# Second expert weights one step later, residual one unit earlier, in a two-block MoE kernel

## The chip, the cores and the metric

The kernel runs on one core of a Trainium2 chip. A time is the device time of one execution in microseconds (us). Three runs of the kernel before gave 2467.74, 2462.54 and 2467.64 us, median 2467.64 us. One further execution was recorded by the hardware profiler, and all rows below are of that one. A difference of less than about 0.2% (4.9 us) can't be told from none.

## The reference

256 tokens of 1024 features go through two blocks of two layers each. In block 1 a layer is a mixer (in one layer a gated delta rule beside sparse attention, in the other gated linear attention) and then a mixture of 32 experts, both with the modulation that comes from a conditioning vector. Block 2 has a token mixer of four branches and again 32 experts, with layer norms, and a residual that is scaled and shifted by rows of a table. Each token picks one of four groups and in it two of eight experts. Cut to what matters, a mixture computes:

```
def expert_block(args):
    xi, e = args
    hid = jax.nn.silu(xi @ w1[e]) * (xi @ w3[e])
    return hid @ w2[e]
yb = lax.map(expert_block, (xb, blk_exp))
y = jnp.zeros((t, d)).at[buf_tok].add(yb * buf_w[:, None])
```

w1 and w3 of an expert are its *first weights*, w2 its *second weights*. All is in float32. In block 1 an expert is 512 wide (first weights 4 MiB, second 2 MiB), in block 2 it is 256 wide (2 MiB and 1 MiB).

## The kernel before, in words

Both mixtures are the function moe (`experts_1` calls it with nf = 512 and centred false, `experts_2` with nf = 256 and centred true). The stages follow one another: mixer, experts_1, mixer, experts_1 (block 1), then mixer, experts_2, mixer, experts_2 (block 2). Every expert is computed, for the tokens that chose it, up to a fixed number of places. The 32 experts go in 11 *units*: five of two experts with 64 places each, five of four experts with 32 places, and a last one of two experts. So 128 places fill the 128 partitions in each unit.

A unit does this. `first` loads the first weights (tiles on queue SP named A); PE multiplies the gathered tokens xg with them (L1023, the *s1* matmuls, written s1(n) for unit n); ACT and DVE make the hidden row (L1026, L1027) and PE turns it (L1036) into ht. In experts_1 this comes in two steps u = 0, 1, each with half of the unit's experts; in experts_2 it is one step. `outer` loads the second weights (tiles named B), and `second` multiplies ht with them in two halves of 512 columns (L932), from which ACT takes yh (L934) and DVE yl (L935). `combine` adds yh and yl back to the tokens' rows in PSUM (L945, PT is the 0/1 matrix of places). `back` prepares that matrix and the weights ws (L953 to L961), and `fetch` gathers the tokens of a later group (L878).

All weights pass through one ring of slots of 1 MiB, taken in rotation by `scratch`; a load waits until the slot's former content has been used, and loads are issued in the order in which they are written, on SP's queue, with at most eight outstanding. In experts_1 the ring has 22 slots, in experts_2 18. `hold` takes a slot out of the rotation for as long as the stage lasts: `keep` for the gates or the residual, and in experts_1 `held` for an accumulator.

The order of loads in experts_1 before: A of step 0, A of step 1, B, all of unit n. In experts_2: A(n), then B(n-1). The unit `turn = len(units) - 2` (the last of four experts, called t below; l is the one behind it, the last) holds an If: `overfull` (L767) computes the tokens that found no place, and its branch is entered only when a count read from memory exceeds 64. Every engine passes the If, and before it SP waits for its outstanding loads. What stands ahead of the If before: in experts_2 the rest of unit t-1 (its B, both halves of second, its combine), in both the two held slots, the first weights of unit t (`begun`), two scratch slots and one for hT, and `residual`. In experts_1 `residual` makes gate rows and clears the accumulator; in experts_2 it is `residual_2`, which loads two rows of the table lnp, half a MiB each, broadcast over the partitions (L170 w<-lnp), and computes with them on DVE (L1942, L1943).

The written order is a start: a scheduler settles the order of instructions on each engine from the dependences between tiles.

Of the kernel before, what the change touches and what calls it, by code (L numbers as in the profile page):

```python
# [811 lines left out]
def moe(c, ctx, index, scale, shift, w13, w2, nf, spare, centred, residual, end):  # L812
# [19 lines left out]
    p = c.pool(ctx, "moe")  # L832
# [88 lines left out]
    prev = None  # L921
# [41 lines left out]
    def experts(unit):  # L963
        e0, ne, _ = unit
        return [e0 + i if e0 < fixed else ranks.expert(e0 + i) for i in range(ne)]

    def first(who, u):

        per = len(who) // steps_of
        return c.slots([w13(e) for e in who[u * per:u * per + per]], [128, 8, 512 if centred else 1024])  # L970

    def outer(pr, who):
        pr["w2"] = c.slots([w2(e) for e in who], [128, 2, 4 * nf])

    turn = len(units) - 2
    for g, us in enumerate(groups):
        if g:
            P, xg = nxt[:2]
        nxt = group(groups[g + 1], False) if g + 1 < len(groups) else (None, None, [])
        share = -(-len(nxt[2]) // len(us))  # L980
        for unit in us:
            e0, ne, cap = unit
            j = e0 - us[0][0]
            n = units.index(unit)
            last = n == len(units) - 1
            todo = [nxt[2].pop(0) for _ in range(min(share, len(nxt[2])))]
            pr = {"n": n, "unit": unit, "h": []}
            who = experts(unit)
            begun = None
            if n == turn:  # L990

                if centred and prev is not None:
                    outer(prev, experts(prev["unit"]))
                    second(prev, 0)
                    second(prev, 1)
                    combine(prev)
                    prev = None
                keep = c.hold(extra)
                held = None if centred else c.hold(extra)
                begun = first(who, 0)  # L1000
                room, hT = [c.scratch(), c.scratch()], c.scratch()
                hT = hT.rearrange("p (a b) -> p a b", b=256)
                out, gate = residual(mp, keep, room, held)
                count = nc.values_load(cnt[0:1, 0:1], min_val=0, max_val=E * CAP,
                                       skip_runtime_bounds_check_because="counts of tokens")
                overfull(c, sp, None if centred else c.tok, scale, shift, out, w, pos, count, nf, *spare, gate, room,
                         hT, ranks)
                c.loaded = None
                who = experts(unit)
            if last:  # L1010
                c.ordered = True
            pr["yh"] = p.tile([128, 2, 512], F32R, name="yh", tag="yy", bufs=2)
            pr["yl"] = p.tile([128, 2, 512], F32R, name="yl", tag="yy", bufs=2)
            per = ne // steps_of
            for u in range(steps_of):
                ws = begun if begun is not None and u == 0 else first(who, u)
                q = sp.tile([128, 512], F32, name="s1")
                for k in range(8):
                    for i in range(128 // cap):

                        m, o = (i, 0) if centred else (i // 2, i % 2)
                        e = j + u * per + m
                        nc.tensor.matmul(q[cap * i:cap * i + cap, :], xg[:, k, e * cap:(e + 1) * cap],  # L1023
                                         ws[m][:, k, 512 * o:512 * o + 512], start=k == 0, stop=k == 7)
                hid = p.tile([128, 256], F32, name="hid", bufs=2)
                nc.scalar.activation(hid, q[:, 0:256], AF.Silu)  # L1026
                nc.vector.tensor_mul(hid, hid, q[:, 256:512])  # L1027
                half = len(todo) // 2
                for f in todo[:half] if u == 0 else todo[half:]:
                    f()  # L1030
                if centred and prev is not None:
                    outer(prev, prev["who"])
                    second(prev, 0)
                q = mp.tile([128, 512], F32, name="ms")
                for ch in range(2):
                    nc.tensor.transpose(q[:, ch * 128:(ch + 1) * 128], hid[:, ch * 128:(ch + 1) * 128], c.id)  # L1036
                ht = p.tile([128, 2, 128], F32, name="ht", bufs=4)
                nc.scalar.activation(ht, q[:, 0:256].rearrange("p (a b) -> p a b", b=128), AF.Copy)
                pr["h"].append(ht)
            pr["who"] = who  # L1040
            if last and not centred:

                for t in range(2):
                    nc.vector.tensor_add(c.x[:, t], c.x[:, t], out[:, t])
            if centred:
                for f in todo[half:]:
                    f()
                if prev is not None:
                    second(prev, 1)
                back(pr, j)  # L1050
                if prev is not None:
                    combine(prev)
            else:
                outer(pr, who)
                back(pr, j)
                if last:
                    combine(prev)
                else:
                    second(pr, 0)
                    if prev is not None:  # L1060
                        combine(prev)
                    second(pr, 1)
            prev = pr
    if centred:
        outer(prev, prev["who"])
    c.ordered = False
    c.table(second(prev, 0))
    combine(prev, (0,))
# [835 lines left out]
def experts_1(c, l):  # L1904

    nc, x = c.nc, c.x
    with ExitStack() as ctx:
        def residual(mp, keep, room, held):
            dg = room[0][:, 0:512].rearrange("p (a b) -> p a b", b=128)
            for hf in range(2):  # L1910
                rows(c, dg, mp, c.mod[:, l, 40 + 4 * hf:44 + 4 * hf], keep[:, hf * 512:hf * 512 + 512], tag=("ms", 2))
            nc.gpsimd.memset(held, 0.0)
            return held.rearrange("p (t d) -> p t d", t=2), keep[:, 0:1024]

        a1 = c.a["A1"][l].rearrange("(q i) p (k c) -> q i p k c", i=2, c=1024)
        b1 = c.a["B1"][l].rearrange("(q i) p (h f c) -> q i f p h c", i=2, h=2, f=4)

        def w1_of(pr, i, j, f):
            o = (f // 2) * 512 + j * 256 + (f % 2) * 128
            return a1[bass.ds(pr, 1), i, :, :, o:o + 128].rearrange("q p k c -> p (q k) c")  # L1920

        def w2_of(pr, i, f):
            return b1[bass.ds(pr, 1), i, f].rearrange("q p h c -> p (q h) c")

        def end(room, gate, y):
            for hf in range(2):
                for t in range(2):
                    o = (2 * t + hf) * 512
                    d = room[:, o:o + 512]
                    nc.vector.tensor_mul(d, y[t][hf], gate[:, hf * 512:hf * 512 + 512])  # L1930
                    nc.vector.tensor_add(x[:, t, hf * 512:hf * 512 + 512], x[:, t, hf * 512:hf * 512 + 512], d)
        moe(c, ctx, l, c.gain, c.mod[:, l, 24:32], lambda e: expert(c.a["A1"][l], e),
            lambda e: expert(c.a["B1"][l], e), 512, (w1_of, w2_of), False, residual, end)
# [12 lines left out]
def experts_2(c, l):  # L1946

    nc, x = c.nc, c.x
    with ExitStack() as ctx:
        a2 = c.a["A2"][l].rearrange("(q i) p (k c) -> q i p k c", i=2, c=512)  # L1950
        b2 = c.a["B2"][l].rearrange("(q i) p (h f c) -> q i f p h c", i=2, h=2, f=2)

        def w1_of(pr, i, j, f):
            o = j * 256 + f * 128
            return a2[bass.ds(pr, 1), i, :, :, o:o + 128].rearrange("q p k c -> p (q k) c")

        def w2_of(pr, i, f):
            return b2[bass.ds(pr, 1), i, f].rearrange("q p h c -> p (q h) c")

        def residual(mp, keep, room, held):  # L1960
            out = keep.rearrange("p (t d) -> p t d", t=2)
            residual_2(c, [room[0][:, 0:1024], room[0][:, 1024:2048]], l, 0, out)
            return out, None

        def end(room, keep, y):
            last(c, c.pool(ctx, "post"), l, keep, y)
        o = l * 32
        moe(c, ctx, 2 + l, c.vec("lnc")[:, o:o + 8], c.vec("lnc")[:, o + 8:o + 16],
            lambda e: expert(c.a["A2"][l], e),
            lambda e: expert(c.a["B2"][l], e), 256, (w1_of, w2_of), True, residual, end)  # L1970
# [317 lines left out]
```

## Time and profile before

| what | us |
|---|---|
| median of three runs | 2467.64 |
| the profiled execution | 2457.6 |
| its span, first to last instruction | 2455.8 |
| PE busy in the span | 2159.5 |
| DVE busy | 886.6 |
| ACT busy | 749.9 |

The profiled execution is 1.8 us longer than its span. PE is TensorE, PEld its loading of weights, DVE VectorE, ACT ScalarE, SP the engine whose queue issues the loads; a q behind a name (PEq, SPq) is that engine's sequencer. A row of the timeline gives start, duration, engine, line, operation, tiles and count of records, and in brackets the idle time before it and what ended that. A matmul in float32 leaves two records. Lines are those of the kernel before; behind the change the same code stands some lines higher (L1023 is L1018, L1036 is L1025, L1942 is L1925).

### The profile page before, as it was taken

The numbers are of one execution on the slowest core, as the hardware profiler recorded it, in microseconds if no ns is written. First come the engines' busy times: TensorE is split into PE (matmuls) and PEld (weight loads), VectorE is DVE, ScalarE is ACT, GpSimd is POOL, SyncE is SP. The second block draws the span as 40 slices with busy tenths as digits, with TensorE's granted clock in tenths as the row PEclk, the third lists the DMA queues.
The fourth block names the chain that finished last, engine by engine and source line by source line (L and its number), as shares of the span: only waits on it lengthen the run. The fifth ranks groups of instructions, "written<-read, shape, count | busy, mean of one in ns | idle before, by whom it ended". The sixth has DMA issues, their size and how long they took to land. (4 is left out here: it accounts for less than half of the span.)

```text
span 2455.8 us, 32737 instructions
## 1 busy us (share of the span) xinstructions
PE 2159.5 (88%) x12546; PEld 1229.3 (50%) x12546; DVE 886.6 (36%) x1983; ACT 749.9 (31%) x1493; POOL 44.6 (2%) x48
## 2 busy tenths in 40 slices
PE   7998899987778989999777798998996899999975
PEld 4667644322224864443222287995432678974322
DVE  3864511110003763111001254973111547861113
ACT  3642311211103452221111154562221445642211
POOL 0001000000000200000000000000000000000000
PEclk8999899999989999999998998998998989989998
DMA  9976569999999356899999971555999924549995
GB/s 393 407 272 284 219 271 400 422 421 422 421 384 419 112 207 255 369 401 421 421 421 383 421 288 47 190 196 223 377 417 379 370 86 142 189 155 356 414 417 234
DMA packets 119845, 775.11 MB, mean 316 GB/s; under 512 B 14185, under 2 KB 15593, under 8 KB 35450
## 3 DMA queue, kind: packets, MB, share of 16 engines
q1 hardware_dynamic: 119674, 772.85, 78.7%
q8 instruction: 105, 1.72, 0.3%
q14 instruction: 66, 0.54, 0.1%
HBM read 771.75 MB, written 1.05 MB: 315 GB/s over the span
## 5 line engine op out<-in xcount | busy, mean ns | idle before, releaser
L1023 PE MATMUL s<-w,xg 128*32 128x512 f32 (+1 forms) x3072 | 612.8, 627 | 94.9 <-DMA w<-A 53.7
L932 PE MATMUL s<-w,ht 128*32 128x512 f32 (+1 forms) x1536 | 348.8, 603 | 38.5 <-DMA w<-B 37.3
L1023 PEld LDWEIGHTS s<-w,xg 128*32 128x32 f32 (+1 forms) x3072 | 140.9, 122 | 384.9 <-issue 265.2
L396 PE MATMUL pj<-hi,wh 128*128 128x256 f32 x864 | 242.6, 283 | 3.4 <-ACT sg L1817 2.4
L397 PE MATMUL pj<-lo,wh 128*128 128x256 f32 x864 | 242.1, 282 | 0.0
L398 PE MATMUL pj<-hi,wl 128*128 128x256 f32 x864 | 239.4, 282 | 0.0
L935 DVE SCALAR_TENSOR_TENSOR yl<-s,ws,yh 128x512 fp32r<-128x512 f32 x88 | 66.0, 750 | 434.3 <-ACT yh L934 416.4
L932 PEld LDWEIGHTS s<-w,ht 128*32 128x32 f32 (+1 forms) x1536 | 83.3, 120 | 219.5 <-issue 137.3
L391 ACT ACTIVATE wh<-w 128x512 fp32r<-128x512 f32 x248 | 154.2, 630 | 117.6 <-PE pj L397 90.4
L392 DVE TENSOR_TENSOR wl<-w,wh 128x512 fp32r<-128x512 f32 x248 | 167.2, 689 | 47.7 <-ACT wh L391 43.8
L934 ACT ACTIVATE yh<-s,ws 128x512 fp32r<-128x512 f32 x88 | 60.5, 687 | 371.6 <-PE s L932 355.4
L396 PEld LDWEIGHTS pj<-hi,wh 128*128 128x128 f32 x864 | 164.9, 191 | 10.4 <-ACT sg L1817 2.8
L398 PEld LDWEIGHTS pj<-hi,wl 128*128 128x128 f32 x864 | 163.2, 191 | 5.0 <-issue 2.1
L397 PEld LDWEIGHTS pj<-lo,wh 128*128 128x128 f32 x864 | 165.2, 191 | 0.1
L1027 DVE TENSOR_TENSOR hid<-hid,s 128x256 f32<-128x256 f32 x66 | 27.7, 420 | 361.6 <-ACT hid L1026 361.5
L1026 ACT ACTIVATE hid<-s 128x256 f32<-128x256 f32 x66 | 25.4, 384 | 430.6 <-PE s L1023 430.3
L359 DVE TENSOR_TENSOR wl<-w,wh 128x512 fp32r<-128x512 f32 (+2 forms) x164 | 111.5, 689 | 97.2 <-ACT wh L358 83.4
L358 ACT ACTIVATE wh<-w 128x512 fp32r<-128x512 f32 (+2 forms) x164 | 99.8, 615 | 112.9 <-PE pj L344 54.3
L886 ACT ACTIVATE xg<-ms,mod,gain 128x128 f32<-128x128 f32 x160 | 72.6, 458 | 170.7 <-PE ms L878 170.7
L878 PEld LDWEIGHTS ms<-P,x 128*128 128x128 f32 x640 | 82.0, 193 | 81.5 <-issue 40.9
L344 PE MATMUL pj<-wl,hi 128*128 128x512 f32 (+2 forms) x272 | 106.4, 393 | 0.0
L343 PE MATMUL pj<-wh,hi 128*128 128x512 f32 (+2 forms) x272 | 101.8, 402 | 2.7 <-ACT rt L412 1.6
(638 smaller groups left out, 2736.5 us busy)
## 6 DMA issues: line engine op xcount, KB each, us to landing
w<-A SPq DMA_DIRECT2D x384, 1024.0 KB, 17.7
w<-B SPq DMA_DIRECT2D x128, 1024.0 KB, 19.8
w<-B SPq DMA_DIRECT2D x128, 512.0 KB, 10.8
w<-ada SPq DMA_DIRECT2D x48, 1024.0 KB, 10.6
w<-wi SPq DMA_DIRECT2D x48, 1024.0 KB, 8.2
w<-w SPq DMA_DIRECT2D x26, 1024.0 KB, 15.7
w<-wo SPq DMA_DIRECT2D x16, 1024.0 KB, 6.0
w<-wbr SPq DMA_DIRECT2D x8, 1024.0 KB, 5.0
```

Of the source, the lines that this page charges most:

```text
L343: nc.tensor.matmul(qs[t][:, :n], a, wh[:, :n], start=s, stop=False)
L344: nc.tensor.matmul(qs[t][:, :n], a, wl[:, :n], start=False, stop=False)
L358: nc.scalar.activation(wh[:, :n], w[:, k], AF.Copy)
L359: nc.vector.tensor_sub(wl[:, :n], w[:, k], wh[:, :n].bitcast(F32))
L391: nc.scalar.activation(wh, w[:, k], AF.Copy)
L392: nc.vector.tensor_sub(wl, w[:, k], wh.bitcast(F32))
L396: nc.tensor.matmul(d, wh[:, e], hi, start=k == 0 and ch % 2 == 0, stop=False, skip_group_check=True)
L397: nc.tensor.matmul(d, wh[:, e], lo, start=False, stop=False, skip_group_check=True)
L398: nc.tensor.matmul(d, wl[:, e], hi, start=False, stop=k == nk - 1, skip_group_check=True)
L878: nc.tensor.matmul(q, src[i][:, t, k * 128:(k + 1) * 128], P[:, t, :m], start=start and t == 0, stop=stop and t == 1, skip_group_check=True)
L932: nc.tensor.matmul(q[cap * i:cap * i + cap, :], ht[:, o * cap:o * cap + cap], pr["w2"][i][:, half, f * 512:f * 512 + 512], start=f == 0, s ...
L1023: nc.tensor.matmul(q[cap * i:cap * i + cap, :], xg[:, k, e * cap:(e + 1) * cap], ws[m][:, k, 512 * o:512 * o + 512], start=k == 0, stop=k ...
```

## The change

In both mixtures the second weights of the unit before are loaded and used behind the first step of the next unit, in experts_1 thus between its two steps, and at the unit of the If too, where they now stand behind the If. The residual, the gates, the held slots and their loads come one unit ahead of the If, with one scratch slot of their own.

```
--- before.py
+++ after.py
@@ -987,26 +987,21 @@
             pr = {"n": n, "unit": unit, "h": []}
             who = experts(unit)
             begun = None
-            if n == turn:
-
-                if centred and prev is not None:
-                    outer(prev, experts(prev["unit"]))
-                    second(prev, 0)
-                    second(prev, 1)
-                    combine(prev)
-                    prev = None
+            if n == turn - 1:
+
                 keep = c.hold(extra)
                 held = None if centred else c.hold(extra)
+                out, gate = residual(mp, keep, c.scratch(), held)
+            if n == turn:
                 begun = first(who, 0)
                 room, hT = [c.scratch(), c.scratch()], c.scratch()
                 hT = hT.rearrange("p (a b) -> p a b", b=256)
-                out, gate = residual(mp, keep, room, held)
                 count = nc.values_load(cnt[0:1, 0:1], min_val=0, max_val=E * CAP,
                                        skip_runtime_bounds_check_because="counts of tokens")
                 overfull(c, sp, None if centred else c.tok, scale, shift, out, w, pos, count, nf, *spare, gate, room,
                          hT, ranks)
                 c.loaded = None
-                who = experts(unit)
+                who, prev["who"] = experts(unit), experts(prev["unit"])
             if last:
                 c.ordered = True
             pr["yh"] = p.tile([128, 2, 512], F32R, name="yh", tag="yy", bufs=2)
@@ -1025,44 +1020,32 @@
                 hid = p.tile([128, 256], F32, name="hid", bufs=2)
                 nc.scalar.activation(hid, q[:, 0:256], AF.Silu)
                 nc.vector.tensor_mul(hid, hid, q[:, 256:512])
-                half = len(todo) // 2
-                for f in todo[:half] if u == 0 else todo[half:]:
-                    f()
-                if centred and prev is not None:
-                    outer(prev, prev["who"])
-                    second(prev, 0)
                 q = mp.tile([128, 512], F32, name="ms")
                 for ch in range(2):
                     nc.tensor.transpose(q[:, ch * 128:(ch + 1) * 128], hid[:, ch * 128:(ch + 1) * 128], c.id)
                 ht = p.tile([128, 2, 128], F32, name="ht", bufs=4)
                 nc.scalar.activation(ht, q[:, 0:256].rearrange("p (a b) -> p a b", b=128), AF.Copy)
                 pr["h"].append(ht)
-            pr["who"] = who
-            if last and not centred:
-
-                for t in range(2):
-                    nc.vector.tensor_add(c.x[:, t], c.x[:, t], out[:, t])
+                if u == 0 and prev is not None:
+                    outer(prev, prev["who"])
+                    second(prev, 0)
+                half = len(todo) // 2
+                for f in todo[:half] if u == 0 else todo[half:]:
+                    f()
+                if u == 0 and prev is not None:
+                    second(prev, 1)
+                    combine(prev)
             if centred:
                 for f in todo[half:]:
                     f()
-                if prev is not None:
-                    second(prev, 1)
-                back(pr, j)
-                if prev is not None:
-                    combine(prev)
-            else:
-                outer(pr, who)
-                back(pr, j)
-                if last:
-                    combine(prev)
-                else:
-                    second(pr, 0)
-                    if prev is not None:
-                        combine(prev)
-                    second(pr, 1)
+            pr["who"] = who
+            if last and not centred:
+
+                for t in range(2):
+                    nc.vector.tensor_add(c.x[:, t], c.x[:, t], out[:, t])
+            back(pr, j)
             prev = pr
-    if centred:
-        outer(prev, prev["who"])
+    outer(prev, prev["who"])
     c.ordered = False
     c.table(second(prev, 0))
     combine(prev, (0,))
@@ -1906,7 +1889,7 @@
     nc, x = c.nc, c.x
     with ExitStack() as ctx:
         def residual(mp, keep, room, held):
-            dg = room[0][:, 0:512].rearrange("p (a b) -> p a b", b=128)
+            dg = room[:, 0:512].rearrange("p (a b) -> p a b", b=128)
             for hf in range(2):
                 rows(c, dg, mp, c.mod[:, l, 40 + 4 * hf:44 + 4 * hf], keep[:, hf * 512:hf * 512 + 512], tag=("ms", 2))
             nc.gpsimd.memset(held, 0.0)
@@ -1959,7 +1942,7 @@
 
         def residual(mp, keep, room, held):
             out = keep.rearrange("p (t d) -> p t d", t=2)
-            residual_2(c, [room[0][:, 0:1024], room[0][:, 1024:2048]], l, 0, out)
+            residual_2(c, [room[:, 0:1024], room[:, 1024:2048]], l, 0, out)
             return out, None
 
         def end(room, keep, y):
```

SP's queue at the start of experts_1 in the first layer, before (wo is the mixer's last weight):

```order
L170 DMA w<-wo 128x2048 x4
L170 DMA w<-A 128x2048 x8
L170 DMA w<-B 128x2048
L170 DMA w<-A 128x2048
L170 DMA w<-B 128x2048 x3
L170 DMA w<-A 128x2048 x7
L170 DMA w<-B 128x2048 x4
```

and now:

```order
L170 DMA w<-wo 128x2048 x4
L170 DMA w<-A 128x2048 x9
L170 DMA w<-B 128x2048
L170 DMA w<-A 128x2048 x3
L170 DMA w<-B 128x2048 x3
L170 DMA w<-A 128x2048 x4
```

The four B loads of the first unit stood behind eight loads of A; they now stand behind the next unit's first four as well, and ahead of its second step.

PE in the same place, before (s_2833 and s_2882 are the two steps of the second unit, s_2799 and s_2810 the halves of the first unit's second weights):

```order
L1023 MATMUL s_2833<-w,xg 64x512 x2
L932 MATMUL s_2799<-w,ht 64x512 x7
L878 MATMUL ms<-P,x 128x128 x4
L1023 MATMUL s_2882<-w,xg 64x512 x13
L932 MATMUL s_2810<-w,ht 64x512 x8
L878 MATMUL ms<-P,x 128x128 x2
L1036 MATMUL ms<-ident,hid 128x128 x2
L1023 MATMUL s_2882<-w,xg 64x512 x3
```

and now (s_2803 and s_2894 are the steps, s_2863 is the second half):

```order
L1018 MATMUL s_2803<-w,xg 64x512 x4
L945 MATMUL y<-yh,PT 128x512 x2
L932 MATMUL s_2863<-w,ht 64x512 x8
L945 MATMUL y<-yl,PT 128x512 x2
L1025 MATMUL ms<-ident,hid 128x128 x2
L878 MATMUL ms<-P,x 128x128 x2
L1018 MATMUL s_2894<-w,xg 64x512 x11
```

The second half of the first unit stood behind 13 of the 16 matmuls of the second unit's second step; it stands ahead of all of them now.

DVE ahead of the If of the last experts_2, before (the two lines L1942 and L1943 are the work on the lnp rows):

```order
L935 SCALAR_TENSOR_TENSOR yl_17830<-s2_18083,ws_17955,yh_17829 128x512
L935 SCALAR_TENSOR_TENSOR yl_17978<-s2_18149,ws_18101,yh_17977 128x512
L935 SCALAR_TENSOR_TENSOR yl_17978<-s2_18160,ws_18101,yh_17977 128x512
L1942 SCALAR_TENSOR_TENSOR w_18179<-x_89,w_18196 128x1024 x2
L1943 SCALAR_TENSOR_TENSOR w_18179<-w_18196,w_18179 128x1024 x2
L1004 TENSOR_LOAD rcnt_17017
L767 COMPARE_AND_BRANCH
```

and now:

```order
L1925 SCALAR_TENSOR_TENSOR w_18004<-x_89,w_18005 128x1024 x2
L935 SCALAR_TENSOR_TENSOR yl_17709<-s2_17946,ws_17840,yh_17708 128x512
L1926 SCALAR_TENSOR_TENSOR w_18004<-w_18005,w_18004 128x1024 x2
L1022 TENSOR_TENSOR hid_18063<-hid_18063,s1_18030 128x256
L935 SCALAR_TENSOR_TENSOR yl_17857<-s2_18083,ws_17990,yh_17856 128x512
L959 TENSOR_SCALAR PT_18142<-ms_18139 128x256
L961 TENSOR_REDUCE ws_18144<-ms_18139 128x1
L953 TENSOR_TENSOR Pw_18628<-P_18146,kw_17054 128x256
L935 SCALAR_TENSOR_TENSOR yl_17857<-s2_18106,ws_17990,yh_17856 128x512
L999 TENSOR_LOAD rcnt_17044
L767 COMPARE_AND_BRANCH
```

The work on the rows was the last thing ahead of the If; it now stands ahead of the hidden row of unit t-1, around the second half of an earlier unit.

PE behind the same If, before:

```order
L767 UNCONDITIONAL_BRANCH
L1023 MATMUL s_18417<-w,xg 32x512 x32
L1036 MATMUL ms<-ident,hid 128x128 x2
L878 MATMUL ms<-P,xh 128x128 x2
L878 MATMUL ms<-P,xl 128x128 x2
L1023 MATMUL s_18533<-w,xg 64x512 x6
```

and now (s_18456 is the first half of unit t-1's second weights):

```order
L767 UNCONDITIONAL_BRANCH
L945 MATMUL y<-yl,PT 128x512 x2
L1018 MATMUL s_18403<-w,xg 32x512 x32
L932 MATMUL s_18456<-w,ht 32x512 x8
L1025 MATMUL ms<-ident,hid 128x128 x2
L878 MATMUL ms<-P,xh 128x128 x2
```

The second weights of unit t-1 were used ahead of the If; they are used behind s1(t) now.

## Rows read from the trace of the kernel before

**Rows 1.** The page's first part: span, busy time and share of each engine

```profile
span 2455.8 us, 32737 instructions
...
PE 2159.5 (88%) x12546; PEld 1229.3 (50%) x12546; DVE 886.6 (36%) x1983; ACT 749.9 (31%) x1493; POOL 44.6 (2%) x48
```

**Rows 2.** Windows: stretch, length, busy PE, PEld, DVE, ACT, POOL, clock, DMA share, GB/s

```profile
320.00:340.00 20.00, 19.90 (x93) 8.28 (x93) 3.14 (x10) 5.33 (x13) 0.00 (x0) 1.00 0.52 208
600.00:620.00 20.00, 14.51 (x78) 3.56 (x76) 1.50 (x2) 1.37 (x2) 0.00 (x0) 1.00 1.01 420
```

**Rows 3.** Waits of PE, whole span: waiting line, releaser, us, times, longest

```profile
PE s L1023 <- DVEq L767: 40.2, 2, 20.4
...
PE y L945 <- PEq L767: 12.1, 2, 6.2
```

**Rows 4.** Timeline of SP's issues ahead of and behind the last If

```profile
2369.39 9.24 SPq L170 DMA_DIRECT2D w<-A  x8
2380.74 2.76 SPq L170 DMA_DIRECT2D w<-lnp  x2
2401.33 2.80 SPq L170 DMA_DIRECT2D w<-A  x4
2404.71 16.43 SPq L170 DMA_DIRECT2D w<-B  x12
```

**Rows 5.** Timeline of PE around and behind the last If

```profile
2383.80 0.73 PE L945 MATMUL y<-yl,PT 128*128 128x512 f32 x2
2404.36 9.06 PE L1023 MATMUL s<-w,xg 128*32 128x512 f32 x64 [19.82 <-DVEq L767]
...
2424.12 1.91 PE L932 MATMUL s<-w,ht 128*32 128x512 f32 x12
...
2435.55 3.65 PE L932 MATMUL s<-w,ht 128*64 128x512 f32 x14
...
2441.79 0.73 PE L945 MATMUL y<-yl,PT 128*128 128x512 f32 x2 [0.78 <-DVE yl L935]
```

**Rows 6.** Timeline of DVE at the last If

```profile
2399.41 2.36 DVE L1942 SCALAR_TENSOR_TENSOR w<-x,w 128x1024 f32<-128x1024 f32 x2 [15.67 <-SPq L767]
```

**Rows 7.** Line L767 from 2300 us: count, min/median/max ns, first and last start

```profile
L767 SPq EVENT_SEMAPHORE  x8: 17/17/17, 2393.1 to 2400.7; - x8
...
L767 PEldq COMPARE_BRANCH  x1: 6070/6070/6070, 2384.2 to 2384.2; - x1
...
L767 DVEq EVENT_SEMAPHORE  x1: 21/21/21, 2404.1 to 2404.1; - x1
```

**Rows 8.** DMA, 2360 to 2440 us in slices of 2 us

```profile
GB/s 410 408 408 410 408 412 408 422 418 426 418 418 430 422 406 422 430 401 385 168 0 217 373 324 418 418 416 414 414 410 399 410 416 406 416 317 18 0 0 0
```

**Rows 9.** Timeline of PE behind the If of the first experts_2

```profile
1886.04 8.81 PE L1023 MATMUL s<-w,xg 128*32 128x512 f32 x64 [20.38 <-DVEq L767]
...
1918.82 3.65 PE L932 MATMUL s<-w,ht 128*64 128x512 f32 x16
```

**Rows 10.** DMA, 1850 to 1950 us in slices of 2.5 us

```profile
GB/s 411 406 419 428 416 423 419 419 419 419 408 385 111 69 367 410 429 411 323 357 411 421 411 406 422 426 422 423 419 419 423 423 426 413 419 423 398 400 421 426
```

**Rows 11.** DMA, 280 to 440 us in slices of 4 us

```profile
GB/s 119 150 160 426 201 0 262 262 352 414 426 379 8 0 225 303 0 35 367 422 428 428 416 418 422 426 426 418 426 414 422 420 393 135 412 422 426 428 420 422
```

**Rows 12.** Waits of SP's queue, 280 to 440 us: us, times, longest

```profile
SPq L170 <- PE s L932: 43.8, 8, 10.2
```

**Rows 13.** Timeline of PE in the first units of experts_1

```profile
312.60 7.08 PE L1023 MATMUL s<-w,xg 128*64 128x512 f32 x30
...
346.52 3.97 PE L932 MATMUL s<-w,ht 128*64 128x512 f32 x15
...
377.93 3.97 PE L932 MATMUL s<-w,ht 128*64 128x512 f32 x15
```

**Rows 14.** Timelines of the mixer behind the first experts_2: SP, then PE

```profile
1908.35 11.08 SPq L170 DMA_DIRECT2D w<-wi  x8
...
1945.36 0.28 PE L396 MATMUL pj<-hi,wh 128*128 128x256 f32 x1
```

More of the change, by code (lines that the diff above doesn't have):

```diff
@@ L1039, in moe @@
                 pr["h"].append(ht)
+                if u == 0 and prev is not None:
[7 more added lines that the diff above has]
+                    combine(prev)
+            if centred:
+                for f in todo[half:]:
+                    f()
             pr["who"] = who
@@ L1044, in moe @@
                     nc.vector.tensor_add(c.x[:, t], c.x[:, t], out[:, t])
-            if centred:
-                for f in todo[half:]:
-                    f()
-                if prev is not None:
-                    second(prev, 1)
-                back(pr, j)
-                if prev is not None:
-                    combine(prev)
-            else:
-                outer(pr, who)
-                back(pr, j)
-                if last:
-                    combine(prev)
-                else:
-                    second(pr, 0)
-                    if prev is not None:
-                        combine(prev)
-                    second(pr, 1)
+            back(pr, j)
             prev = pr
-    if centred:
-        outer(prev, prev["who"])
+    outer(prev, prev["who"])
     c.ordered = False
```

## The prediction

> **What bounds the kernel now.** I read the page's first part, then windows of 20 us, then PE's waits, then the two ends of the expert stages. PE is busy for 88% of 2455.8 us [rows 1], which invites the guess that PE sets the time. The windows correct this: at 600 us, in the middle of an expert stage, PE is busy for 14.51 of 20 us while the DMA share is 1.01 at 420 GB/s [rows 2]. There the weights set the pace: one slot (1 MiB, 1.049 MB) takes 1.049 / 0.420 = 2.5 us. So a PE microsecond in the middle of such a stage is worth nothing, and what counts is (a) time in which the queue of loads stands still, and (b) what PE still has to do after the last weights are in.
>
> (a) stands at the start of experts_1: from 320 to 340 us PE is busy for 19.90 of 20 and the DMA share is 0.52 [rows 2]. In slices of 4 us the six from 328 to 352 read 8, 0, 225, 303, 0, 35 GB/s instead of 422 [rows 11]: 4 x (6 - 571/422) = 18.6 us of loads lost. The queue was waiting on PE: 43.8 us in eight waits for L932, the longest 10.2 [rows 12]. The second layer of block 1 starts with the same code and units, and I count it alike.
>
> (b) stands at the end of experts_2. PE waits there twice, 40.2 us in all, on DVE's way into the If [rows 3], 19.82 us of it in the last layer [rows 5] and 20.38 in the first [rows 9]. DVE in turn sat 15.67 us until its lnp rows came, at 2399.41 [rows 6]; these two half-MB loads are issued at 2380.74, behind the eight loads of A(t) [rows 4]. (t is the unit of the If, l the last; A and B are the first and second weights.) After the wait PE works without a real pause to 2442.5: s1(t) from 2404.36, B(l) until 2435.55 + 3.65 = 2439.2 [rows 5]. The loads were in before that: in slices of 2 us the bytes end at 2431.6 [rows 8], and the last of them are the closing lnp rows, 1.049 MB = 2.5 us, so B(l) was there at 2429.1. PE was done with it 10 us later.
>
> **The change part by part.**
>
> *experts_2, order at the If.* Removed ahead of the If: 8 half-MB loads of B(t-1), 4 MiB = 4 x 2.5 = 10.0 us, with second(t-1) and its combine on PE. They are added behind it; the sum of bytes is equal. The lnp rows move a unit ahead, but stay ahead of the If, so they don't alter when its last load lands. The queue waits for its eight outstanding loads in the If (2393.1 to 2400.7 [rows 7]); with 10.0 us fewer bytes ahead that ends at 2390.7. The hole that this drain leaves (168, 0, 217, 373, 324 GB/s [rows 8], 4.8 us) stays as it is: nothing that is moved fills it. So the bytes end at 2431.6 again and B(l) lands at 2429.1 again.
>
> DVE's two pairs on the rows (2.36 us for the first pair [rows 6], the second like it) now stand between two yl of an earlier unit. If the rows are late there, DVE and then PE wait; but the rows are issued before A(t-1), so they land before PE can start s1(t-1) anyway, with 8 loads (20 us) behind them. I take 0; bounds 0 and 4.7 us a layer.
>
> PE then: s1(t) starts some 10 us earlier (2394 instead of 2404.36), with second(t-1) behind it, and the rest is paced by landings: B(t-1), A(l), B(t), B(l). B(t) is in 2 slots before B(l): 2429.1 - 5.0 = 2424.1. After that PE owes the last half of second(t), 1.91, four pairs of its combine at 0.73 and second(l), 3.65 [rows 5]: 8.5 us, ending at 2432.6, with B(l) landing meanwhile. Before it ended at 2439.2: **-6.6**.
>
> First layer: the bytes stop near 1880.7 and run again from the equivalent of 1884.9 (111, 69, 367 GB/s from 1880 [rows 10]). A(l), B(t) = 8 slots later is 1906 (20 us, and one of ramp), plus 8.5 is 1914.5; before, second(l) ended at 1918.82 + 3.65 = 1922.5 [rows 9]: **-8.0**. This has to survive the mixer that follows. Its wi loads are issued from 1908.35 on and are in by about 1935, and PE's first use in the long row of projections is at 1945.36 [rows 14]: 8 us earlier is 1937.4, so they are still there, with little to spare. I take all of it; bounds 0 and -8.0.
>
> *PE's branch.* PE's own branch takes 6070 ns at 2384.2 [rows 7], hidden now in the 19.82 us. It is shown as the wait of the instruction behind it at the two other Ifs, 12.1 us in two [rows 3]. After the change it hides behind A(t)'s landing only if PE gets to it before 2390.7 - 6.1 = 2384.6; what PE does ahead of it ends when B(t-2) is used, before A(t) is all in by 8 loads (20 us). So I take 0; at the other end it stands on the path in both layers, 12.1, and the -14.6 of experts_2 shrinks to -2.5, the sum to -16.5 (2451); that goes with R1 below, 0.03 of its chance. [...]
>
> *experts_1, order of loads.* Now A(n,0), A(n,1), B(n); then A(n,0), B(n-1), A(n,1), used in that order. Nothing is added: 12 loads in a unit of two experts as before. What changes is when PE frees B(0)'s slots relative to what stands in the ring behind them. Before, PE takes B(0)'s second half at 346.52, after A(1,0) and 13 of the 16 matmuls of A(1,1); after, it is ahead of A(1,1). PE is the bound in this stretch, and slots that are free behind a blocked one can't be filled. One step of 16 matmuls lasts about 7.1 us (30 records, 7.08 [rows 13]). So the block should end that much earlier and 7 us of the 18.6 be returned: **-7 a layer, -14**. Bounds: 0 (the ring fills elsewhere) and -18.6 a layer. Below nothing: A(n,0) and B(n-1) now alternate, so A(n,1) waits for a slot of B; one wait of the longest kind is 10.2 [rows 12]. The units after 416 us have the DMA as bound, and I count them at 0: B(n) had 31.4 us of a unit (346.52 to 377.93 [rows 13]) and needs less.
>
> *Residual, gates, held in experts_1.* Made one unit earlier, by the same instructions; two slots leave the 22 of the ring one unit sooner. PE does not wait for DVE at the Ifs of experts_1 (the two such waits [rows 3] are those of experts_2 above), so nothing is won or lost: 0, bounds -2 and +5 (two slots' loads).
>
> **Sum.** -6.6 - 8.0 - 14 = -28.6. The profiled execution took 2457.6 us, 1.8 more than its span [rows 1]; it would take 2429.0. The median shown, 2467.64, lies 10.0 above the profiled one, so on that footing 2467.6 - 28.6 = **2439**.
>
> **Rivals.**
> *R1, only the ends of experts_2 gain.* The hole at the start of experts_1 closes at one place and opens at another, because PE is the bound there whatever the queue does: 19.90 of 20 us speak for it, the eight waits on L932 against. 2467.6 - 14.6 = 2453; if the mixer also takes the first layer's 8.0, 2461.
> *R2, the whole hole closes.* With B behind the next step the queue never stands behind L932 in experts_1: -2 x 18.6 - 14.6 = -51.8, 2416. Against it: the ring is 22 slots, and it also waits for L1023 there.
> *R3, hidden anyway.* PE's wait on DVE turns into a wait on B(t-1), A(l) and B(t) behind the drain, and the ends come when they came; the projections after the first layer wait for wi; experts_1 as R1. 0 to -3: 2465 to 2468. For it: the bytes end at the same time. Against: PE begins the long part of second(l) at 2435.55 [rows 5], 6.4 us after B(l) landed.
> *R4, slower: the ring of experts_1.* A(n,1) now stands behind B(n-1), whose slots come free only after the next unit's first step; if the queue so gets two more waits of 10.2 us in each layer, 4 x 10.2 - 14.6 = +26, 2494. It decides from 14.6 / 10.2 = 1.4 such waits on. Against: B(n-1) is used earlier in relation to what is loaded after it, not later.
> That the change doesn't do what it says I give nothing: the order on SP, DVE and PE shows every move.
>
> **How the numbers follow.** Forecast 0.50, R1 0.19, R2 0.09, R3 0.12, R4 0.10. What can be told from no change is 0.2%, 4.9 us. Faster: forecast, R1, R2 = 0.78; same: R3 = 0.12; slower: R4 = 0.10. Forecast, R1, R3 and half of R2 lie in 2424 to 2468, some 0.85 with the doubt of the sum; the forecast's own range is 2430 to 2450.
>
> **What would show it.** Right: PE's two waits on DVE at L767 gone and in their place waits on w<-A and w<-B; second(l) ending within 4 us of B(l)'s landing in the last layer; the lnp rows landing before A(t-1); the sum of SP's waits on PE's second matmuls from 280 to 440 us below 43.8, and the slices from 328 to 352 with 7 us more at 422 GB/s. Wrong: holes of DMA at the start of experts_1 of 18 us again (R1), none at all (R2), or holes in its middle, where it is at 420 GB/s now (R4); or a last layer in which PE starts s1(t) at 2404 again (R3).

## The result and the profile after

The changed kernel takes 2427.95 us (median of 4 runs, 2425.86 to 2429.93) against 2465.99 us before (4 runs, 2462.54 to 2467.74); the ratio is 0.9847 with a 95% interval of 0.983 to 0.9864, so 38 us less. 2439 was forecast, with a range of 2424 to 2468; 2428 lies near the lower end of it, and 2 us below the 2430 to 2450 that the prediction gave for the forecast by itself. The profiled execution after took 2428.4 us with a span of 2426.6, close to its median.

The profiled execution of before was some 8 us quicker than its runs. To see where the time went, I cut both spans at the router's first matmul (L648) and the last combine of each expert stage. E1 and e2 below each contain two of before's expert stages, so they show what these take in another execution:

| stretch, us | before | after | same code in e1 or e2 |
|---|---|---|---|
| first experts_1 | 476.4 | 461.7 | 475.8 (e2) |
| second experts_1 | 474.2 | 464.0 | 477.1 (e2) |
| first experts_2 | 250.7 | 246.9 | 253.0 (e1) |
| mixer behind it | 266.8 | 268.7 | 267.0 (e1) |
| second experts_2 | 250.6 | 247.2 | 253.0 (e1) |
| everything else | 737.1 | 738.1 | |

So experts_1 gives some 14 us a layer and experts_2 some 6, of which the mixer takes 2 back.

The page's first part after, answering to [rows 1]:

```profile
span 2426.6 us, 32734 instructions
...
PE 2149.3 (89%) x12546; PEld 1230.8 (51%) x12546; DVE 885.9 (37%) x1983; ACT 751.9 (31%) x1493; POOL 44.9 (2%) x48
```

No engine does much less: PE's busy time falls by 10.2 us of 2159.5. The start of experts_1 in the same windows and slices as [rows 2, 11, 12], first the window, then DMA in slices of 4 us from 280, then SP's waits from 280 to 440:

```profile
320.00:340.00 20.00, 20.00 (x90) 7.51 (x90) 3.24 (x9) 4.83 (x11) 0.00 (x0) 1.00 1.00 397
```

```profile
GB/s 143 125 184 78 0 0 254 426 420 422 424 426 424 352 358 420 422 428 424 418 408 383 424 426 420 426 424 422 293 264 412 426 426 426 422 416 369 401 428 424
```

```profile
SPq L170 <- PE s L1018: 79.8, 31, 7.0
SPq L753 <- DVE kidx L726: 14.2, 1, 14.2
SPq L170 <- PE s L932: 12.9, 4, 4.0
```

And SP's waits before the change, on the first matmuls from 280 to 440, then all from 325 to 355 us, around the hole:

```profile
SPq L170 <- PE s L1023: 40.2, 9, 14.0
...
SPq L170 <- PE s L1023: 14.0, 1, 14.0
SPq L170 <- PE s L932: 13.0, 2, 10.2
```

PE is as busy as before (20.00 of 20 us), but the DMA share beside it is 1.00 instead of 0.52. The hole of [rows 11] from 328 to 352 is gone; one from 292 to 308 has become longer. Counting 4 x (1 - rate/422) for each slice below 422, loading stood still for 40.7 us between 280 and 440 before, and for 26.0 now: 14.7 less, and the stage is 14.7 shorter. SP's waits on the second matmuls fell from 43.8 to 12.9 us; it waits longer on the first ones (79.8 instead of 40.2), in 31 short pieces. The hole of before was one wait of 14.0 us on a first matmul and then two on second ones, 10.2 of them on the second half.

The longer hole from 292 to 308, 5 us more than before, is a price of the new order. The next loads in the queue are now first weights of the third unit, and that is the first unit whose experts are known only at run time: SP must read their numbers (L753) from a row that DVE writes (kidx), and this read waited 14.2 us. Before, loads of the second unit's B stood there, which need no such read; two of them were issued from 289.42 on.

At the last If, PE's waits over the whole span, answering to [rows 3]; then PE, DVE and SP in order of time, answering to [rows 4 to 6]:

```profile
PE s L1018 <- DMA w<-A: 59.8, 55, 2.3
PE s L932 <- DMA w<-B: 43.0, 41, 4.1
...
PE ms L1025 <- PEq L767: 9.6, 2, 5.0
...
PE s L1018 <- SPq L767: 6.1, 5, 1.4
```

```profile
2351.64 0.70 PE L945 MATMUL y<-yl,PT 128*128 128x512 f32 x2 [0.27 <-PEq L767]
2352.27 1.66 PE L1018 MATMUL s<-w,xg 128*32 128x512 f32 x6
2355.36 3.63 PE L1018 MATMUL s<-w,xg 128*32 128x512 f32 x28 [1.43 <-SPq L767]
...
2365.25 5.33 PE L1018 MATMUL s<-w,xg 128*32 128x512 f32 x26 [0.56 <-SPq L767]
...
2402.59 1.92 PE L932 MATMUL s<-w,ht 128*32 128x512 f32 x14
...
2406.76 3.65 PE L932 MATMUL s<-w,ht 128*64 128x512 f32 x16
```

```profile
2319.30 2.35 DVE L1925 SCALAR_TENSOR_TENSOR w<-x,w 128x1024 f32<-128x1024 f32 x2
2321.57 0.74 DVE L935 SCALAR_TENSOR_TENSOR yl<-s,ws,yh 128x512 fp32r<-128x512 f32 x1
2322.24 2.35 DVE L1926 SCALAR_TENSOR_TENSOR w<-w 128x1024 f32<-128x1024 f32 x2
```

```profile
2336.62 9.22 SPq L170 DMA_DIRECT2D w<-A  x8
2366.44 5.91 SPq L170 DMA_DIRECT2D w<-B  x8
2372.93 3.18 SPq L170 DMA_DIRECT2D w<-A  x4
2377.71 19.75 SPq L170 DMA_DIRECT2D w<-B  x12
```

The two waits of 20 us on DVE are gone; PE is behind the If at 2351.5, 14 us before SP's eight loads are all in (2365.5), and does s1(t) piece by piece as A(t) lands. DVE works on the rows at 2319 with no wait. Line L767 and the slices of 2 us from 2330, answering to [rows 7, 8]:

```profile
L767 SPq EVENT_SEMAPHORE  x8: 17/17/17, 2355.3 to 2365.5; - x8
...
L767 PEldq COMPARE_BRANCH  x1: 443/443/443, 2351.0 to 2351.0; - x1
```

```profile
GB/s 416 399 416 404 416 410 430 420 414 430 410 422 406 418 426 381 143 8 70 252 236 401 365 328 416 432 426 430 422 412 406 412 403 418 401 418 401 418 352 59
```

The hole at the drain has grown: 143, 8, 70, 252, 236, 401, 365, 328 lose 2 x (1 - rate/418) each, with the 381 ahead of them 7.5 us in all, against 5.0 by the same count before [rows 8].

### The profile page after: what moved, and what is told of

The parts are those of the page before. It is cut to its first block, busy times and chain, and to the rows that moved or that the text cites. A ratio compares the mean times of both kernels' runs of the same rounds, so it can differ in the third digit from the quotient of the medians.

```text
span 2426.6 us, 32734 instructions
## 1 busy us (share of the span) xinstructions
PE 2149.3 (89%) x12546; PEld 1230.8 (51%) x12546; DVE 885.9 (37%) x1983; ACT 751.9 (31%) x1493; POOL 44.9 (2%) x48
## 5 line engine op out<-in xcount | busy, mean ns | idle before, releaser
L932 PE MATMUL s<-w,ht 128*32 128x512 f32 (+1 forms) x1536 | 348.4, 617 | 44.8 <-DMA w<-B 43.0
L932 PEld LDWEIGHTS s<-w,ht 128*32 128x32 f32 (+1 forms) x1536 | 82.6, 122 | 224.5 <-issue 138.5
L878 PEld LDWEIGHTS ms<-P,x 128*128 128x128 f32 x640 | 85.3, 197 | 66.5 <-issue 35.8
L878 PE MATMUL ms<-P,x 128*128 128x128 f32 x640 | 103.7, 294 | 2.0 <-issue 1.6
## 6 DMA issues: line engine op xcount, KB each, us to landing
w<-B SPq DMA_DIRECT2D x128, 512.0 KB, 10.2
```

What stands on the lines that cost most here:

```text
L878: nc.tensor.matmul(q, src[i][:, t, k * 128:(k + 1) * 128], P[:, t, :m], start=start and t == 0, stop=stop and t == 1, skip_group_check=True)
L932: nc.tensor.matmul(q[cap * i:cap * i + cap, :], ht[:, o * cap:o * cap + cap], pr["w2"][i][:, half, f * 512:f * 512 + 512], start=f == 0, s ...
```

## The experiments

**Each stage alone.** Two kernels, the one with only experts_1 changed, the other with only experts_2 (the loop takes the path of before or of after by `centred`):

```
new = not centred     # e1;   new = centred   # e2
```

> Only experts_1 is changed (order of loads, gates one unit early); experts_2 is as before. Theory A (most of the gain is experts_1's hole in the loads, 14.8 and 10.2 us in the two stages by the traces): about -25 us, 2441. Theory B (the shares of the forecast, 14 and 14.6): -14, 2452. If experts_1 carries all of what the run medians moved: -36 to -38, 2428.

> Only experts_2 is changed (second weights behind the If, rows one unit early); experts_1 is as before. Theory A: -4 to -7 us, 2460, PE's two waits of 20 us on DVE gone all the same. Theory B: -14.6, 2451. Rival (the hole behind the If, 7 us instead of 5 in both layers, takes it all back): 0, 2466.

E1 measured 2439.37 us, ratio 0.9893 (0.9877 to 0.9908), 26.6 below the 2465.96 of before beside it; e2 measured 2454.24, 0.9947 (0.9934 to 0.9961), 11.7 below. They add up to 38.3, the whole. Theory A's 25 for experts_1 is confirmed. Its 4 to 7 for experts_2, read from the traces, is too low, since before's trace was a quick one; 11.7 lies between A and B.

**The two parts of experts_2's change.** In both, experts_1 is as after.

```
if n == turn and centred:               # e3: B(t-1) stays ahead of the If
    outer(prev, experts(prev["unit"])); second(prev, 0); second(prev, 1); combine(prev); prev = None
...
out, gate = residual(mp, keep, room[0], held)      # e4, centred only: at the If, behind begun
```

> As the changed kernel, but in experts_2 the second weights of unit t-1 stay ahead of the If; the rows still come one unit early. Theory A (the hole is longer because half-MB loads are the first ones behind the If): the hole is back at about 5 us, PE no longer waits on DVE for the rows, and the kernel is 2 to 5 us faster than the changed one, 2424. Theory B (moving the second weights is what brings PE to the end in time): 7 us slower than the changed one, 2435.

> As the changed kernel, but in experts_2 the residual and its rows are made at the If as before; the second weights of unit t-1 stay behind it. Theory A: PE waits on DVE again for 8 to 20 us at both Ifs, but the end is paced by the loads; 0 to 3 us slower than the changed one, 2429 to 2431. Rival (the wait on DVE is what counted): all of experts_2's gain is lost, 5 to 7 us slower, 2434.

E3: 2432.59 us, 0.9863 (0.9848 to 0.9878), experts_2 248.6 and 247.7 in its profile. E4: 2430.56 us, 0.9863 (0.9848 to 0.9878), experts_2 246.8 and 246.4. PE's waits at the Ifs, e3 and then e4:

```profile
PE y L945 <- PEq L767: 12.0, 2, 6.0
PE ms L1047 <- PEq L767: 9.8, 2, 4.9
PE s L1032 <- SPq L767: 2.8, 2, 1.4
```

```profile
PE s L1032 <- DVEq L767: 42.7, 4, 20.6
PE ms L1047 <- PEq L767: 8.2, 2, 4.8
```

In e4 PE waits 20 us at each If again, as before the change, and the stage is as short as after, as theory A had it. So with the second weights behind the If that wait costs nothing. In the order of before it does cost: e3, which takes only that wait away, gets most of the gain too (253.0 in e1 to 248.6 and 247.7). Each part alone brings PE to the end in time, and the other then adds little: the gains don't add. Neither theory on e3 holds as it stands. It doesn't beat the changed kernel, though its hole is shorter (356, 66, 37, 291 GB/s, 4.4 us); that PE stands 6 us in its branch there, with second(t-1) ahead of it, would explain this, but was not tried by itself. And of the 4.6 us by which its median is above the changed kernel's, only 2.2 lie in experts_2 in the profiled executions; 2.8 lie in the first experts_1, whose code is the same.

**Which units of experts_1.** E5 keeps the new order for the first unit only, e9 for units 0 to 3, e10 for units 4 and later; the others have their second weights behind their own second step, as before (in e9 and e10 their gathering of later tokens stays where it is after the change; e5 writes the same choice with other names).

```
pr["later"] = centred or n < 4      # e9;   n < 1: e5;   n >= 4: e10
owed = prev is not None and prev["later"]
...
if not pr["later"]:
    outer(pr, who)       # then back, second(pr, 0), combine(prev) if not owed, second(pr, 1)
```

> As the changed kernel, but in experts_1 only the first unit's second weights are loaded and used behind the next unit's first step; all later units have the order of before (both steps' first weights, then the unit's own second weights). Theory A (only the start of the stage, where PE is the bound and the ring is blocked, gains): experts_1 within 2 us of the changed kernel in each layer, total 2428 to 2432. Theory C (each unit's order gains a little): most of experts_1's 26.6 us is lost, about 2450.

> As the changed kernel, but in experts_1 only units 0 to 3 (two experts each) have their second weights behind the next unit's first step; from unit 4 on the order is that of before. Theory L (PE is the bound through the five units of two experts, then the loads are; what counts is how far the loads are ahead when this turns, so the order of the last such units and not of the first): most of the 26.6 us of experts_1 is lost, 2448 to 2456, as with the first unit alone (2455.9). Theory S (what is lost is the hole at 328 to 352 us, wherever the stage goes then): all is kept, 2428 to 2432. Theory C (each unit a share): half, 2438 to 2446.

> The other way round: units 0 to 3 as before, from unit 4 on the new order. Theory L: nearly all is kept, 2428 to 2434, although the slices from 328 to 352 us show the hole of before again. Theory S: nearly all is lost, about 2452. Theory C: half, 2438 to 2446.

E5: 2455.85 us, 0.9968 (0.9959 to 0.9977), so its theory A, 2428 to 2432, fell. E9: 2471.55, 1.0039 (1.0026 to 1.0053); it also loads and uses the last unit's second weights a second time, 4 MiB or some 10 us in each experts_1 at the 420 GB/s of [rows 2], so 2451 to 2452 belong to the order. E10: 2437.75, 0.9895 (0.988 to 0.991). DMA in slices of 4 us, e5 and e10 from 280, e9 from 440:

```profile
GB/s 195 70 213 426 147 12 250 305 403 408 424 358 197 106 317 403 412 428 432 422 365 248 430 428 426 418 422 426 365 4 35 408 82 66 395 424 418 428 422 426
```

```profile
GB/s 100 168 123 430 233 0 258 229 365 420 424 393 14 266 258 4 201 420 428 426 422 424 420 426 424 414 424 420 416 422 424 248 412 424 428 420 422 424 416 424
```

```profile
GB/s 420 424 422 424 156 254 270 0 289 424 426 426 422 414 416 422 424 422 418 424 426 420 422 416 426 418 420 420 426 420 420 422 420 422 416 422 424 420 422 422
```

The hole is not removed by moving the first unit; it goes to where the old order next meets a full ring: 392 to 416 us in e5 (4, 35, 408, 82, 66), 456 to 476 in e9 (156, 254, 270, 0, 289). In both places SP waits on second matmuls, 27.0 us in three waits (e5, 385 to 420 us) and 19.5 in two (e9, 450 to 480). All three theories miss something. L fell with e10, which has the right order at the turn from PE to the loads and still gives back half; S fell with e5 and e9; C would give e9 a gain. What fits is plain bookkeeping of the loads, wherever they stand still:

| kernel | stood still 280 to 520, us | against before | first experts_1 | against before |
|---|---|---|---|---|
| before | 41.0 | | 476.4 | |
| after | 26.4 | -14.6 | 461.7 | -14.7 |
| e5 | 42.6 | +1.6 | 478.9 | +2.5 |
| e6 (below) | 28.6 | -12.4 | 465.9 | -10.5 |
| e9, with 10.0 for its extra loads | 49.6 | +8.6 | 484.8 | +8.4 |
| e10 | 33.6 | -7.4 | 468.7 | -7.7 |

The two differences agree within 2 us in all five kernels. The old order costs a hole of 11 to 19 us where it meets a full ring; that is paid about once, not in each unit, and it is all the same where. This is an account of what was lost, not of why a hole has the size it has; what decides that was not tried.

**PE's order against the loads' order.** E6 keeps the order of loads, and only makes PE use the second half of the second weights behind the unit's second step.

```
step = nc.tensor.matmul(...)              # the last one of the step
if u == steps_of - 1 and prev is not None:
    with tc.issue_after(step.ins):        # experts_1 only
        second(prev, 1)
    combine(prev)
```

> As the changed kernel, loads in its order, but in experts_1 PE uses the second half of the second weights behind the unit's second step (16 matmuls, 7 us later) in every unit. Theory A (the loads wait for the slots that PE holds until that second half is done): 5 to 8 us a layer are lost, 2438 to 2444, and SP's waits on PE's second matmuls from 280 to 440 us rise well above 12.9. Theory D (the order of loads alone gains, PE's order doesn't count): 2428.

E6: 2441.76 us, 0.9916 (0.9903 to 0.9929). SP's waits from 280 to 440 in it:

```profile
SPq L170 <- PE s L1018: 48.7, 22, 7.0
SPq L170 <- PE s L932: 33.4, 5, 11.9
```

The waits on second matmuls are 33.4 instead of 12.9, and the stages 465.9 and 468.5 instead of 461.7 and 464.0: in the profiled execution 4 of the 14 us a layer come from taking that second half one step earlier. In the runs it is more. That execution was 4.2 us quicker than e6's median, and the median is 13.8 us above the changed kernel's, 6.9 a layer if all of it lies in experts_1, and inside theory A's 2438 to 2444. So slots are held by PE's use, theory D fell, and this step is worth between 30% and half of the gain of 13 to 14 us a layer; these runs don't settle it closer. The granted clock is 0.94 in all five executions of e6 and 0.95 to 0.96 in the four of after; what part of the 13.8 us that makes is not shown.

**The longer hole.** E7 loads the second weights of unit t-1 in experts_2 as four loads of 1 MiB, e8 those of all units but the last; c2 gathers the last unit's tokens ahead of the If, c1 is e8 and c2 together.

```
if centred and pr["n"] < len(units) - 1:     # e8, c1;   == turn - 1: e7
    pr["w2"] = [c.slot(w2(e), [128, 2, 4 * nf]) for e in who]
...
if n == turn and centred:                     # c1, c2: ahead of begun
    for f in todo:
        f()
    todo = []
```

> As the changed kernel, but in experts_2 the second weights of unit t-1, the first loads behind the If, come as four loads of 1 MiB instead of eight of half a MiB. If the half-size loads make the hole longer (7 us against 5): -2 us a layer, 2424. If the hole is only the drain and the restart: 0, 2428. Second half and first half of these weights now land together, PE may begin second(t-1) up to 5 us later; if that counted at the end, 2432.

> The same for the second weights of all units of experts_2 but the last. If eight outstanding loads of 1 MiB keep the queue fuller than eight of half a MiB throughout: more than the one unit gains, 2420 to 2424. If the rate in the middle (420 GB/s) is the limit whatever the size: as with one unit, 2424 to 2428.

> As the changed kernel, but in experts_2 the gathering of the last unit's tokens (L878, 9 us of PE that stood behind the If) is done ahead of the If, where PE waits for A(t). If the loads pace the end of the stage: 0, 2428. If PE does: -2 to -6 us.

> Both: the gathering ahead of the If, and second weights of experts_2 in loads of 1 MiB (all units but the last). The shorter hole (5 us instead of 7.5) was given back because PE was late behind the If; if that is so, with 9 us less of PE work there it is kept: -2.5 us a layer, 2422 to 2424. If something else took it: 2428 to 2430.

E7: 2436.34 us, 0.9892 (0.9878 to 0.9907). E8: 2429.88, 0.9869 (0.9854 to 0.9885). C2: 2430.34, 0.9871 (0.9856 to 0.9886). C1: 2430.68, 0.9866 (0.9851 to 0.9881). None is faster than the changed kernel's 0.9847. E8 from 2330 us in slices of 2:

```profile
GB/s 426 418 422 422 426 418 418 426 418 414 422 426 418 414 410 426 258 0 94 389 389 418 422 430 422 434 418 434 418 426 418 414 426 401 395 406 416 293 14 0
```

The hole is 258, 0, 94, 389, 389: 4.6 us instead of 7.5, and the bytes end at 2405.4 instead of 2407.7. These are the far ends of what the traces have. With half-MB loads first behind the If (after, e2, e4, e5, e6, e9, e10, c2) the holes of both layers lie between 5.9 and 7.6 us, 6.9 in the mean; with whole ones (e7, e8, c1) between 4.6 and 6.4, 5.3 in the mean. So the half-MB loads do make it longer, by some 1.6 us. But the stage is as long (246.9). E8's last stretch on PE shows why:

```profile
2399.92 1.90 PE L932 MATMUL s<-w,ht 128*32 128x512 f32 x10 [1.45 <-DMA w<-B]
2402.60 0.74 PE L945 MATMUL y<-yh,PT 128*128 128x512 f32 x2 [0.78 <-ACT yh L934]
2403.39 1.92 PE L932 MATMUL s<-w,ht 128*32 128x512 f32 x16
...
2408.89 1.94 PE L932 MATMUL s<-w,ht 128*64 128x512 f32 x8
```

With whole loads the last expert brings both halves at once, so the end of the first half of second(t) and all of the second come after it; with half loads the first half of all four experts is done by then. From the landing of B(t) to the end of second(l) PE takes 10.9 us here, from 2399.92 to 2410.83, and 8.2 after the change, from 2402.2 to 2410.4: what the hole gained goes back at the end. C1, with the gathering out of PE's way as well, gains no more. In e7 the first experts_2 alone is 254.1 against 247.6 in the second, with the same code; from 1868 to 1874 us L878 takes 0.63 us a pair there and L932 3.51 for 10 records, where 0.38 to 0.44 and 1.90 stand in the second layer. The granted clock there, from 1850 to 1870 us, is 0.67, and 0.91 in the same stretch of the changed kernel; from 1870 to 1890 it is 0.91 in e7 as well. Why it was lower in this layer stays open.

## Why the prediction was right, and where it was not

- *The loads set the middle, and only a standing queue or PE's rest at the end costs.* Right: the busy times fell by at most PE's 10 us of 2159.5, and the bookkeeping above accounts for the first experts_1 within 2 us in all five kernels.
- *experts_1, -7 a layer.* The place and the direction were right, the size was not: 26.6 in two layers (e1), 13.3 each. The term took only the step by which PE uses the second half earlier; e6 measures that as 4 us in its profiled execution and 7 in the runs, so for this step it was not far off. What it left out are the two waits of the hole that come before: 14.0 us on a first matmul and 2.8 on the first half of second. They are gone as well. PE is through the first half 10 us earlier (329.96 instead of 339.75), and the next unit's four A loads stand ahead of B; which of the two did it no run separates. The bound of 18.6 was the better price: the slices from 328 to 352 lose 1.3 us now, but 5 more stand at 292 to 308, in SP's read of the experts' numbers, which the prediction doesn't have.
- *experts_2, -14.6.* In the runs 11.7 (e2), so 3 too high. The load of A(t) ended 9 us earlier relative to the stage's start (200.1 instead of 209.2), close to the 10.0 worked out. "The hole that this drain leaves stays as it is" failed: 7.5 us instead of 5.0, since the half-MB loads are now first behind the If; with whole ones at that place (e7) it is 5.0 again. And the end came 10.2 us after the last byte of B(t) by the prediction's count (2407.7 - 7.5 = 2400.2), not 8.5. That is not PE's work: it took the last byte for the landing. The last load of B(t) landed 10.3 us after its issue at 2391.9, at 2402.2, and from there PE needed 8.2; in e8, where PE waits for it, the bytes were in at 2397.9 by the slices and the wait ended at 2399.92.
- *DVE's rows early, 0, and the wait on DVE.* Right that it costs nothing: no wait at 2319. That a wait of 20 us costs nothing when PE is in time at the end was in the argument, and e4 shows it. But the prediction credits the whole of experts_2's gain to the order at the If, and e3 shows that the early rows alone bring 4 to 5 us a layer.
- *PE's branch, 0.* It never came on the path, but not for the reason given: in the two experts_2 it lasted 360 and 443 ns after, not 6070. A packet of 16 KiB on an instruction queue (q8) starts 3.6 us after the branch of 6.07 us and 3.8 us after the one of 443 ns. What made the branch short no run shows; that the packet bears on it isn't shown either, nor that this queue is PE's.
- *The mixer passes on all of the first layer's gain.* Nearly: it takes 2 us (266.8 to 268.7; 269.3 in e2 against 267.0 in e1).
- *Residual, gates, held in experts_1, 0.* Not tried by itself; e5, with all of it and the old order from the second unit on, gains nothing in experts_1.
- *R4, slower.* SP's waits did become more, 31 on the first matmuls, but short, none over 7.0 us.
- The sum, -28.6, agreed with the two traces (-29.2) by luck: errors in both terms cancelled, -14 against -25 in experts_1 and -14.6 against -5.3 in experts_2 with its mixer. The runs moved by 38, since the profiled execution of before was quicker than its runs; there the terms are -14 against -26.6 and -14.6 against -11.7.

## What to carry to other kernels

Where a ring of buffers feeds an engine, count the time in which the queue of loads stands still, in slices, over the whole stretch up to the next load-bound stage: that sum was what the stage gained or lost, wherever the hole stood. A long wait in the table of waits is not a price: the same 20 us of PE waiting cost nothing in e4, and 4 to 5 us in the order of before. Two changes that each bring PE to the end in time give their gain once, not twice. One profiled execution can be off from the runs by as much as a term of the sum (8 us in before, 4 in e6, 6.5 in e10), and the same stage in a second kernel shows it.

## What the runs showed of the hardware

PE's COMPARE_BRANCH at the If took 5.9 to 6.4 us or 0.36 to 0.45 us and nothing between; in c2 the same code gave 6184 ns in the first layer and 356 ns in the second of experts_2. What decides was not tried. At the eight Ifs of before and after a packet of 16 KiB on the instruction queue q8 starts 3.4 to 3.8 us after the start of that branch, at either length. The six long ones end 1.4 to 1.5 us after it is in, the two short ones 4.4 to 4.5 us before.

In e8 the wait of PE on the last B(t) ended 2 us after the load's last byte: at 2399.92, where the slices give 2397.9 for the byte by estimate (they end at 2405.4, less 7.5 us for the three MiB behind it).

Eight loads of half a MiB behind a drained queue reached 252, 236, 401, 365, 328 GB/s in the first 10 us (after), loads of 1 MiB 389, 389, 418, 422 in 8 us (e8); over all traces the holes overlap, as said above.
